# The second layer's seven products: order, transfers and splits set by hand, and small copies ahead of their halves

## The chip, the core and the metric

The kernel runs on one core of a Trainium2 chip. A core has five engines that run side by side, each through its own queue in order: TensorE (PE, matrix products, with weight loads in a sub-queue PEld), VectorE (DVE), ScalarE (ACT), GpSimd (POOL) and SyncE (SP, which here only issues transfers). PE reads SBUF and writes PSUM, eight banks of 128 x 512 fp32; DVE and ACT read the banks. Transfers (DMA) are issued on SP's, POOL's or ACT's queue; those that add to their destination are issued on POOL's. The metric is the device time of one execution in microseconds (us), as a median of several runs.

## The reference

Two layers on x (512 tokens x 1024): a pooling mixer and multi-head latent attention with 16 heads, each gated and projected back, then one RMS norm. What matters here is the second layer's end:

```python
def mla_layer(x, cos, sin, norm_g, w_in, q_norm_g, w_q_b, kv_norm_g, w_kv_b, w_out):
    ...
    o = causal_mla_attention(q_nope, q_rope, k_nope, k_rope, v)
    y = o.reshape(B, S, MLA_WIDTH) * jax.nn.silu(z)
    return x + y @ w_out

def reference(...):
    ...
    return rmsnorm(x, final_norm)
```

`y` is 512 x 2048, `w_out` 2048 x 1024.

## The kernel before

**Precision.** Each fp32 operand is split into a high and a low half (`halves`: ACT copies the rounded value, DVE subtracts it). `mm3` makes one product of three matmuls: high·high, low·high, high·low.

**Attention.** A loop runs over the 16 heads `h`. In the pass of head `h` stand the scores of head `h + 1` (`scores`: per block `i` of 128 queries a bank or part of one, and on DVE a masked row maximum into `mx`), the transposes of head `h`'s weights (`transposes`: three banks, split into `pt_hi`, `pt_lo`; the diagonal corner of keys block 3 is copied whole into `pt_3`), the softmax of head `h + 1`, projections for later heads (`qk`, `vv`) and the values of head `h` (`values`). In `qk` a bank is split into halves and its first 128 columns are also copied whole (`t0`), since block 0 of the scores is made of whole fp32 operands (L988). In `vv` the second bank has such a copy, too (`v3`). Before the change each small copy comes after the halves of its bank. Two engines that read one bank do so one after the other.

**Seven products.** `y @ w_out` is made of seven products in place of eight. `y` (kept transposed) is cut into a11, a12 (first 256 tokens; first and second half of the channels) and a21, a22 (last 256 tokens); `w_out` into B11, B12 (first half of its rows; LEFT and RIGHT columns) and B21, B22. Before, they run in this order:

| | left factor | right factor | banks |
|---|---|---|---|
| 1 | a11 | B11 | `acc` |
| 2 | s1 = a21 − a22 | B11 + B12 (`x_sum`) | `both` |
| 3 | s2 = s1 − a11 | + B22 (`x_sum`) | `acc` |
| 4 | s2 + a12 | B22 (`y_sum`) | `both` |
| 5 | s3 = a11 − a21 | B22 + B12 (`y_sum`) | `acc` |
| 6 | a12 | B21 | `last` |
| 7 | a22 | all four summed (`x_sum`) | `acc` |

Product 1 runs inside the loop, one fourth in each of heads 12 to 15. Each later one is `multiply`: four `part`s of 12 matmuls, the first two with the first strip of the right factor, the last two with the second. `gather` adds a bank to `xs`, the residual rows, between the products that go on in the same bank.

**Sums by transfer.** `Summed.load` loads tiles of `w_out` on SP's queue and adds further quarters to them on POOL's queue. `Summed.strip` then splits a tile set into a strip. A strip takes two of four buffers (tag "w"), so a strip's buffers come free when the product that reads it is half done or done. `x_sum` has eight tiles of 256 KB in buffers of the attention (tags qh, ql, kh, kl): four at head 13 and four at head 14, the latter once the last scores have been made. `y_sum` has four of 512 KB. The left factors' halves lie in two slots that take turns.

**Order.** A planner orders the instructions of each engine by program order and by its own estimate of readiness. Inside `tc.manual_schedule()` each engine takes them as written. Before the change, only `finish` (the squares, norms and the last product's parts) is written under it; the products before it are the planner's.

Of the kernel before, what the change touches and what calls it, by code (L numbers as in the profile page):

```python
# [11 lines left out]
F32 = mybir.dt.float32  # L12
# [3 lines left out]
ALU = mybir.AluOpType  # L16

P = 128
D = 1024
S = 512  # L20
NT = S // P
# [29 lines left out]
def trunk_kernel(  # L51
# [824 lines left out]
    for i in range(3, 8):  # L876
# [13 lines left out]
        base=0,  # L890
# [17 lines left out]
    def projections(p):  # L908

        wq, wkv = strip(pair_parts(p), eng=pool)  # L910
        pairs[p] = st = {}

        def qk(name, i):
            def unit():
                b = bank()
                if name == "q":
                    ws, ks, off = tuple(v[:, :, i * DN : (i + 1) * DN] for v in wq), range(3), 0
                else:
                    ws, ks, off = tuple(v[:, :, i * 256 : i * 256 + DN] for v in wkv), range(2), 3
# [12 lines left out]
                t0 = ap.tile([P, P], F32, name=f"{name}0", tag=f"{name}0", bufs=1)  # L932
                act.activation(t0, b[:, :P], AF.Copy)
                st[name, i] = (th, tl, t0)

            return unit

        def vv(i):
            def unit():
                if i == 0:  # L940
                    st["v"] = tuple(
                        xn_tile(F32R).rearrange("p (t c) -> p t c", t=NT) for n in "hl"
                    )
                b = bank()
                for j in range(2):
# [16 lines left out]
                halves(b[:, : n * 256], vh, vl)  # L962
                if i == 1:
                    st["v3"] = ap.tile([P, 256], F32, name="v3", tag="v3", bufs=1)
                    act.activation(st["v3"], b[:, 256:], AF.Copy)

            return unit

        return [[qk("k", 0), qk("q", 0)], [qk("k", 1), qk("q", 1)], [vv(0), vv(1)]]
# [3 lines left out]
    def scores(h):  # L973
# [42 lines left out]
    def transposes(pm):  # L1016
        for keys in ((0,), (1, 3), (2,)):
            b = bank()
            n = 0
            for j in keys:  # L1020
                for i in range(j, NT):
                    pe.transpose(  # L1022
                        b[:, n : n + P], pm[:, OFF[i] + j * P : OFF[i] + (j + 1) * P], ident
                    )
                    n += P
            n, base = (NT - keys[0]) * P, PT_BASE[keys[0]]
            halves(b[:, :n], pt_hi[:, base : base + n], pt_lo[:, base : base + n])
            if 3 in keys:
                act.activation(pt_3, b[:, n:], AF.Copy)

    def values(h):
        st, i2 = pairs[h // 2], h % 2
# [13 lines left out]


    w_out2 = mla_w_out[0]
    a11, a12, a21, a22 = quarters()
    x_sum, y_sum = Summed(w_out2, 1), Summed(w_out2, 2)  # L1050

    def slot_of(hi, lo):
# [2 lines left out]
            for name, (home, tag) in (("a_hi", hi), ("a_lo", lo))  # L1055
        )

    def sum_tiles(n):

        for i in range(n):  # L1060
            tag = ("qh", "ql", "kh", "kl")[i]
            x_sum.tiles.append(ap.tile([P, 1, S], F32, name="b_x", tag=tag, bufs=2))

    (k0, q0), (k1, q1), vs = projections(0)
    qr = {1: QRope(1)}
# [11 lines left out]
    for h in range(H):  # L1077
        p, odd = divmod(h, 2)
        g, t = divmod(h + 5, 4)
        if h == 12:  # L1080
            slots[1] = slot_of((lp, "t2"), (lp, "q_r"))
            first_half[0] = columns_of(w_out2, 0, LEFT, 0)
            split_tokens(a11, slots[1], (0, 1))
            acc = [bank() for _ in range(2)]
        if h == 13:
            split_tokens(a11, slots[1], (2, 3))
        nxt = scores(h + 1) if h + 1 < H else None
        if h in (13, 14):
            sum_tiles(4)
            x_sum.load(0, LEFT, pieces=range(4 * (h - 13), 4 * (h - 12)))  # L1090
            x_sum.load(0, RIGHT, add=True, pieces=range(4 * (h - 13), 4 * (h - 12)))
        if odd:
            ahead = projections(p + 2) if p + 2 < H // 2 else [[], [], []]
        transposes(sc[0])
# [9 lines left out]
        if h == 14:  # L1104
            slots[0] = slot_of((lp, "latT_hi"), (wk, "q_r"))
            s1 = lp.tile([P, 8, 256], F32, name="s1", tag="latT_lo", bufs=1)
            s1 = [s1[:, 2 * i : 2 * i + 2, :] for i in range(4)]
            s2 = [
                lp.tile([P, 2, 256], F32, name="s2", tag=tag, bufs=1)
                for tag in ("cosT", "sinT", "k_a", "k_b")  # L1110
            ]
            combine(s1, a21, a22, ALU.subtract, range(3))
            split_tokens(s1, slots[0], range(2))
        if h == 15:
            t1 = x_sum.strip(0)
            split_tokens(s1, slots[0], (2,))
            combine(s2, s1, a11, ALU.subtract, range(3))
        values(h)
        if g < 4 and t < 2:
            if t == 0:  # L1120
# [10 lines left out]
        sc = nxt  # L1131


    combine(s1, a21, a22, ALU.subtract, (3,))
    split_tokens(s1, slots[0], (3,))
# [4 lines left out]
    y_sum.load(1, RIGHT)  # L1140
    both = [bank() for _ in range(2)]
    t1 = [t1, x_sum.strip(1)]
    x_sum.load(1, RIGHT, add=True)
    multiply(both, t1, slots[0], True)
    for t in range(2):
        gather(t, LEFT, acc[t])
    combine(s2, s1, a11, ALU.subtract, (3,))
    split_tokens(s2, slots[1])
    multiply(acc, x_sum.strips(), slots[1], False)
    x_sum.load(1, LEFT, add=True)  # L1150
    for t in range(2):
        gather(2 + t, RIGHT, both[t])
    combine(s2, s2, a12, ALU.add)
    split_tokens(s2, slots[0])
    for t in range(2):
        gather(t, RIGHT, acc[t], ALU.subtract)
    multiply(both, y_sum.strips(), slots[0], False)
    y_sum.load(0, RIGHT, add=True)
    g_fin = row(final_norm, D, "g_fin", tag="gain")
    s3 = [  # L1160
        v.rearrange("p (i k c) -> p i k c", i=2, k=2)[:, i]
        for v in (xn_tile(), xn_tile())
        for i in range(2)
    ]
    combine(s3, a11, a21, ALU.subtract)
    split_tokens(s3, slots[1])
    for t in range(2):
        gather(t, RIGHT, both[t])
    multiply(acc, y_sum.strips(), slots[1], False)
    split_tokens(a12, slots[0])  # L1170
    last = [bank() for _ in range(2)]
    multiply(last, [columns_of(w_out2, 1, LEFT, i) for i in range(2)], slots[0], True)
# [5 lines left out]
    junk = lp.tile([P, 512], F32, name="junk", tag="turned", bufs=1)  # L1178
    ssq = {t: [] for t in range(NT)}
    rs = {}  # L1180

# [34 lines left out]
        act.activation(o[t][:, c], o[t][:, c], AF.Copy, scale=rs[t])  # L1216
        send(t, c, queue)

    for t in range(2):
        gather(2 + t, RIGHT, acc[t], ALU.subtract)  # L1220
    split_tokens(a22, slots[1])
    t4 = x_sum.strips()

    def finish():

        for t in range(2):
            square(t, RIGHT)
            square(2 + t, RIGHT)
        for t in range(2):
            gather(t, LEFT, last[t])  # L1230
            total(t)
            square(t, LEFT)
            power(t)
        for t in range(2):
# [22 lines left out]
        normed(3, LEFT)  # L1257

    with tc.manual_schedule():
        finish()  # L1260
    phase.close()

# [36 lines left out]
```

## Time and profile before

| | us |
|---|---|
| median of 3 runs | 721.43 |
| lowest, highest | 720.68, 722.55 |
| the profiled execution | 719.77 |
| its span, first to last instruction | 717.9 |
| PE busy | 701.2 |
| DVE busy | 450.9 |
| ACT busy | 353.6 |
| POOL busy | 137.4 |

The loop over heads starts at about 443 us, product 2 at 641, product 7 at 699.6; PE's last matmul starts at 710.5. In the profile a matmul of 512 columns is shown with 0.39 us, though the next one starts 0.23 us behind it, because matmuls are pipelined. A row of the timeline has start, duration, engine, line, instruction, output and inputs, shapes and a count; in brackets stands the engine's idle time before it and what ended it. A row of the windows has, for each stretch, its length, busy time (and count) of PE, PEld, DVE, ACT, POOL, then the granted clock of PE as a share of full speed, the DMA share and GB/s.

### The profile page before, as it was taken

The page shows a single profiled execution, that of the slowest core. Times are in us where ns is not written, and L with a number is a line of the kernel's source. Part 1 is how long each engine was busy: PE and PEld are TensorE (multiplying, and loading weights), DVE is VectorE, ACT ScalarE, POOL GpSimd, SP SyncE. Part 2 cuts the span into 40 slices and gives each one's busy share as a digit, 9 for nine tenths or more (in the row PEclk, how much of TensorE's full clock was granted, in tenths as well). Part 3 has the DMA queues.
Part 4 walks back from the last instruction along what each step waited for, and adds up shares of the span by engine and source line. Part 5 has one row for each costly group of instructions (what it writes and reads, how often), then busy time and mean ns, then how long its engine had stood idle before and what let it go on. Part 6 is the DMA issues. An engine that isn't in the chain of part 4 may idle for free.

```text
span 717.9 us, 10034 instructions
## 1 busy us (share of the span) xinstructions
PE 701.2 (98%) x3529; PEld 597.8 (83%) x3529; DVE 450.9 (63%) x883; ACT 353.6 (49%) x765; POOL 137.4 (19%) x182
## 2 busy tenths in 40 slices
PE   8999999999999999999999999999999999999896
PEld 7888888888888888799888888898888888877685
DVE  5964453463587897651634212686776887788885
ACT  6462242232243565554642334665575576555662
POOL 5000000000001440154600005221223021054302
PEclk9999999999999999999999999999999999999998
DMA  8341331332355996134432514123132143599813
GB/s 263 120 135 62 115 114 63 118 98 78 111 171 123 238 198 136 57 110 131 118 112 67 155 52 125 53 50 84 53 95 59 38 126 122 114 222 212 153 44 119
DMA packets 69539, 82.79 MB, mean 115 GB/s; under 512 B 12144, under 2 KB 45936, under 8 KB 69488
## 3 DMA queue, kind: packets, MB, share of 16 engines
q1 hardware_dynamic: 60448, 65.10, 30.3%
q0 software_dynamic: 8896, 16.78, 13.3%
q8 instruction: 28, 0.46, 0.3%
q10 hardware_dynamic: 144, 0.26, 0.1%
q14 instruction: 23, 0.19, 0.1%
HBM read 75.83 MB, written 2.10 MB: 109 GB/s over the span
## 4 chain that ended last, share of the span: by engine, by line
PE 87%; DVE 5%; DMA 4%; ACT 2%; issue 1%; POOL 1%; POOLq 0%; SPq 0%; ACTq 0%
PE bank L185 26%; PE bank L184 26%; PE bank L183 26%; DMA b_x<-in_mla_w_out 3%; PE bank L1022 2%; PE bank L301 2%; PE bank L985 2%; PE bank L986 1%; DMA b_y<-in_mla_w_out 1%; DVE a_lo L189 1%; PE bank L988 1%; PE bank L226 1%; ACT pm L1008 1%; DVE pm L1014 1%; DVE w_lo L560 1%
## 5 line engine op out<-in xcount | busy, mean ns | idle before, releaser
L166 ACT ACTIVATE w_hi<-raw 128x512 fp32r<-128x512 f32 (+2 forms) x200 | 105.0, 576 | 130.0 <-PE bank L184 119.7
L167 DVE TENSOR_TENSOR w_lo<-raw,w_hi 128x512 fp32r<-128x512 f32 x132 | 86.6, 691 | 114.0 <-ACT w_hi L166 114.0
L183 PE MATMUL bank<-h_hi,w_hi 128*128 128x512 f32 x368 | 143.6, 390 | 0.0
L185 PE MATMUL bank<-h_lo,w_hi 128*128 128x512 f32 x368 | 143.4, 390 | 0.0
L184 PE MATMUL bank<-h_hi,w_lo 128*128 128x512 f32 x368 | 143.4, 390 | 0.0
L167 POOL TENSOR_TENSOR w_lo<-raw,w_hi 128x256 fp32r<-128x256 f32 (+2 forms) x68 | 61.3, 931 | 193.5 <-ACT w_hi L166 193.4
L185 PEld LDWEIGHTS bank<-h_lo,w_hi 128*128 128x128 f32 x368 | 69.1, 188 | 14.3
L183 PEld LDWEIGHTS bank<-h_hi,w_hi 128*128 128x128 f32 x368 | 69.1, 188 | 14.3
L184 PEld LDWEIGHTS bank<-h_hi,w_lo 128*128 128x128 f32 x368 | 69.1, 188 | 14.2
L183 PE MATMUL bank<-w_hi,h_hi 128*128 128x512 f32 (+1 forms) x176 | 64.6, 367 | 0.0
L184 PE MATMUL bank<-w_hi,h_lo 128*128 128x512 f32 (+1 forms) x176 | 64.2, 365 | 0.0
L185 PE MATMUL bank<-w_lo,h_hi 128*128 128x512 f32 (+1 forms) x176 | 64.2, 365 | 0.0
L185 PE MATMUL bank<-w_lo,a_hi 128*128 128x512 f32 (+1 forms) x116 | 44.7, 386 | 2.8 <-DVE w_lo L560 2.8
L183 PE MATMUL bank<-w_hi,a_hi 128*128 128x512 f32 (+1 forms) x116 | 44.6, 385 | 0.0
L184 PE MATMUL bank<-w_hi,a_lo 128*128 128x512 f32 (+1 forms) x116 | 44.5, 383 | 0.0
L559 ACT ACTIVATE w_hi<-b_x 128x512 fp32r<-128x512 f32 (+1 forms) x40 | 30.6, 798 | 24.8 <-DMA b_x<-in_mla_w_out 9.3
L183 PE MATMUL bank<-latT_hi,w_hi 128*128 128x512 f32 x104 | 42.3, 407 | 0.0
L185 PE MATMUL bank<-latT_lo,w_hi 128*128 128x512 f32 x104 | 40.7, 391 | 0.0
L184 PE MATMUL bank<-latT_hi,w_lo 128*128 128x512 f32 x104 | 40.7, 391 | 0.0
L992 DVE CUSTOM_DVE_ANT_0 pm<-bank,mask 128x128 f32<-128x128 f32 (+2 forms) x64 | 30.5, 489 | 14.8 <-PE bank L185 10.7
L560 DVE TENSOR_TENSOR w_lo<-b_x,w_hi 128x512 fp32r<-128x512 f32 (+1 forms) x40 | 34.3, 902 | 6.1 <-ACT w_hi L559 5.9
L185 PEld LDWEIGHTS bank<-w_lo,h_hi 128*128 128x128 f32 x176 | 33.1, 188 | 4.4
(204 smaller groups left out, 1405.7 us busy)
## 6 DMA issues: line engine op xcount, KB each, us to landing
raw<-in_pool_w_in SPq DMA_DIRECT2D x64, 256.0 KB, 3.1
raw<-in_mla_w_in SPq DMA_DIRECT2D x32, 256.0 KB, 3.3
b_x<-in_pool_w_out POOLq DMA_DIRECT2D x12, 512.0 KB, 7.5
b_x<-in_mla_w_out POOLq DMA_DIRECT2D x24, 256.0 KB, 7.9
raw<-in_mla_w_q_b SPq DMA_DIRECT2D x36, 128.0 KB, 2.4
raw<-in_pool_w_group SPq DMA_DIRECT2D x16, 256.0 KB, 2.6
q_r<-stack SPq DMA_DIRECT2D x64, 64.0 KB, 2.0
raw<-in_mla_w_kv_b SPq DMA_DIRECT2D x16, 256.0 KB, 2.9
```

The source lines that it names most:

```text
L166: act.activation(hi, raw, AF.Copy)
L167: ins = eng.tensor_tensor(lo, raw, f32(hi), ALU.subtract)
L183: pe.matmul(o, a[0], b[0], start=start, stop=False, skip_group_check=more)
L184: pe.matmul(o, a[1], b[0], start=False, stop=False, skip_group_check=more)
L185: pe.matmul(o, a[0], b[1], start=False, stop=stop, skip_group_check=more)
L189: dve.tensor_tensor(lo, src, f32(hi), ALU.subtract)
L301: pe.matmul(first[i][:, c], w0.views[0][a][:, k, i * P : (i + 1) * P], (h_hi, h_lo)[b][:, k, c], start=k == 0 and n == 0, stop=k == KD - 1 ...
L559: act.activation(hv[:, k, :], raw, AF.Copy)
L560: eng.tensor_tensor(lv[:, k, :], raw, f32(hv[:, k, :]), ALU.subtract)
L985: pe.matmul(o, q_r[h // 4][:, h % 4, c], k_a[:, :n], start=True, stop=False)
L992: dve.tensor_tensor_reduce(out=pm[:, OFF[i] : OFF[i] + w], in0=o[:, :w], in1=mask[:, S - w :], scale=1.0, scalar=-3.0e38, op0=ALU.add, op1 ...
L1022: pe.transpose(b[:, n : n + P], pm[:, OFF[i] + j * P : OFF[i] + (j + 1) * P], ident)
```

## The change

Four things change.

- In `qk`, `vv` and `transposes` the small whole copy on ACT comes ahead of `halves`.
- `scores` takes the blocks in the order 1, 2, 3, 0.
- Products 2 to 7 are written in `products()`, under `manual_schedule` together with `finish`, in the order 2, 6, 3, 4, 5, 7 of the table. s3 and s2 are formed in place, in a21's and a11's storage, rows 0 to 5 ahead of the block and rows 6 and 7 in it. Splits take four rows (1024 columns) at a time, combines two.
- The sum tiles of `x_sum` lie in qh, ql, kh, kl, and three buffers that the rotary tables and their work had (cosT, sinT, turned): seven are loaded at head 13 and one at head 14. `finish` makes the norms of the first 256 tokens ahead of the gathers that product 7 waits for.

```diff
             def unit():  # qk; likewise vv and transposes
...
-                halves(b[:, c0:], th[:, c0:], tl[:, c0:])
                 t0 = ap.tile([P, P], F32, name=f"{name}0", tag=f"{name}0", bufs=1)
                 act.activation(t0, b[:, :P], AF.Copy)
+                halves(b[:, c0:], th[:, c0:], tl[:, c0:])
...
-        for i in range(NT):
+        for i in (1, 2, 3, 0):
...
+    homes = [(ap, tag, 2) for tag in ("qh", "ql", "kh", "kl")]
+    homes += [(lp, tag, 1) for tag in ("cosT", "sinT", "turned")]
+    homes += [(ap, "qh", 2)]
+    def first_sum(k0, k1):
+        for home, tag, n in homes[k0:k1]:
+            x_sum.tiles.append(home.tile([P, 1, S], F32, name="b_x", tag=tag, bufs=n))
+        x_sum.load(0, LEFT, pieces=range(k0, k1))
+        x_sum.load(0, RIGHT, add=True, pieces=range(k0, k1))
...
+        if h == 13:
+            first_sum(0, 7)
+        if h == 14:
+            first_sum(7, 8)
...
+            combine_rows(s1, a21, a22, ALU.subtract, 0, 6)
+            split_rows(s1, slots[0], 0, 4)
         if h == 15:
+            t1 = [x_sum.strip(0)]
+            split_rows(s1, slots[0], 4, 6)
...
+    combine_rows(a21, a11, a21, ALU.subtract, 0, 6)
+    combine_rows(a11, s1, a11, ALU.subtract, 0, 6)
+    s3, s2 = a21, a11
...
+    def products():
+        combine_rows(s1, a21, a22, ALU.subtract, 6, 8)
+        split_rows(s1, slots[0], 6, 8)
+        x_sum.load(1, RIGHT, add=True, pieces=range(4))
+        t1.append(x_sum.strip(1))
+        x_sum.load(1, RIGHT, add=True, pieces=range(4, 8))
+        multiply(both, t1, slots[0], True)
+        split_rows(a12, slots[1], 0, 4)
+        p2 = [columns_of(w_out2, 1, LEFT, 0)]
+        split_rows(a12, slots[1], 4, 8)
+        p2.append(columns_of(w_out2, 1, LEFT, 1))
+        y_sum.load(1, RIGHT)
+        multiply(last, p2, slots[1], True)
+        for t in range(2):
+            gather(t, LEFT, acc[t])
+            gather(2 + t, RIGHT, both[t])
+        combine_rows(s3, a11, a21, ALU.subtract, 6, 8)
+        combine_rows(s2, s1, a11, ALU.subtract, 6, 8)
+        split_rows(s2, slots[0], 0, 4)
+        split_rows(s2, slots[0], 4, 8)
+        t2 = x_sum.strips()
+        x_sum.load(1, LEFT, add=True)
+        multiply(acc, t2, slots[0], False)
+        for i in (0, 4):
+            combine_rows(s2, s2, a12, ALU.add, i, i + 4)
+            split_rows(s2, slots[1], i, i + 4)
+        y1 = [y_sum.strip(0)]
+        for t in range(2):
+            gather(t, LEFT, last[t])
+        y1.append(y_sum.strip(1))
+        y_sum.load(0, RIGHT, add=True)
+        multiply(both, y1, slots[1], False)
+        for t in range(2):
+            gather(t, RIGHT, acc[t], ALU.subtract)
+        split_rows(s3, slots[0], 0, 4)
+        split_rows(s3, slots[0], 4, 8)
+        y2 = [y_sum.strip(0)]
+        for t in range(2):
+            gather(t, RIGHT, both[t])
+        y2.append(y_sum.strip(1))
+        multiply(acc, y2, slots[0], False)
+        split_rows(a22, slots[1], 0, 4)
+        split_rows(a22, slots[1], 4, 8)
...
     def finish():
+        t4 = [x_sum.strip(0)]
         for t in range(2):
+            square(t, LEFT)
+            total(t)
             square(t, RIGHT)
-            square(2 + t, RIGHT)
-        for t in range(2):
-            gather(t, LEFT, last[t])
-            total(t)
-            square(t, LEFT)
             power(t)
-        for t in range(2):
-            part(acc[t], t4[0], slots[1], 0, t, False, False, True)
             for c in (LEFT, RIGHT):
                 normed(t, c)
+        for t in range(2):
+            gather(2 + t, RIGHT, acc[t], ALU.subtract)
+            square(2 + t, RIGHT)
+            part(acc[t], t4[0], slots[1], 0, t, False, False, True)
+        t4.append(x_sum.strip(1))
         part(acc[0], t4[1], slots[1], 1, 0, False, True, True)
...
     with tc.manual_schedule():
+        products()
         finish()
```

`combine_rows` works on two rows (512 columns) an instruction, `split_rows` on all the rows that it is given.

More of the change, by code (lines that the diff above doesn't have):

```diff
@@ L961, in unit @@
                 )
-                halves(b[:, : n * 256], vh, vl)
                 if i == 1:
@@ L965, in unit @@
                     act.activation(st["v3"], b[:, 256:], AF.Copy)
+                halves(b[:, : n * 256], vh, vl)
             return unit
@@ L1026, in transposes @@
             n, base = (NT - keys[0]) * P, PT_BASE[keys[0]]
-            halves(b[:, :n], pt_hi[:, base : base + n], pt_lo[:, base : base + n])
             if 3 in keys:
                 act.activation(pt_3, b[:, n:], AF.Copy)
+            halves(b[:, :n], pt_hi[:, base : base + n], pt_lo[:, base : base + n])
     def values(h):
@@ L1048, in trunk_kernel, with combine_rows, split_rows @@
     w_out2 = mla_w_out[0]
-    a11, a12, a21, a22 = quarters()
+    a11, a12, a21, a22 = (
+        y[:, half * 8 : half * 8 + 8, t * 256 : (t + 1) * 256] for t in range(2) for half in range(2)
+    )
+    def combine_rows(out, a, b, op, k0, k1):
+        for k in range(k0, k1, 2):
+            dve.tensor_tensor(*(v[:, k : k + 2, :] for v in (out, a, b)), op)
+    def split_rows(src, slot, k0, k1):
+        halves(*(v[:, k0:k1, :] for v in (src, *slot)))
     x_sum, y_sum = Summed(w_out2, 1), Summed(w_out2, 2)
@@ L1056, in slot_of @@
         )
[L1058 to L1062, printed above, removed]
+    homes = [(ap, tag, 2) for tag in ("qh", "ql", "kh", "kl")]
[6 more added lines that the diff above has]
+        x_sum.load(0, RIGHT, add=True, pieces=range(k0, k1))
     (k0, q0), (k1, q1), vs = projections(0)
@@ L1082, in trunk_kernel @@
             first_half[0] = columns_of(w_out2, 0, LEFT, 0)
-            split_tokens(a11, slots[1], (0, 1))
+            split_rows(a11, slots[1], 0, 4)
             acc = [bank() for _ in range(2)]
         if h == 13:
-            split_tokens(a11, slots[1], (2, 3))
+            split_rows(a11, slots[1], 4, 8)
         nxt = scores(h + 1) if h + 1 < H else None
[L1088 to L1091, printed above, removed]
+        if h == 13:
+            first_sum(0, 7)
+        if h == 14:
+            first_sum(7, 8)
         if odd:
@@ L1106, in trunk_kernel @@
             s1 = lp.tile([P, 8, 256], F32, name="s1", tag="latT_lo", bufs=1)
[L1107 to L1113, printed above, removed]
+            combine_rows(s1, a21, a22, ALU.subtract, 0, 6)
+            split_rows(s1, slots[0], 0, 4)
         if h == 15:
-            t1 = x_sum.strip(0)
-            split_tokens(s1, slots[0], (2,))
-            combine(s2, s1, a11, ALU.subtract, range(3))
+            t1 = [x_sum.strip(0)]
+            split_rows(s1, slots[0], 4, 6)
         values(h)
@@ L1131, in trunk_kernel @@
         sc = nxt
-    combine(s1, a21, a22, ALU.subtract, (3,))
-    split_tokens(s1, slots[0], (3,))
+    combine_rows(a21, a11, a21, ALU.subtract, 0, 6)
+    combine_rows(a11, s1, a11, ALU.subtract, 0, 6)
+    s3, s2 = a21, a11
     y_sum.tiles = [
@@ L1139, in trunk_kernel @@
     ]
-    y_sum.load(1, RIGHT)
     both = [bank() for _ in range(2)]
-    t1 = [t1, x_sum.strip(1)]
-    x_sum.load(1, RIGHT, add=True)
-    multiply(both, t1, slots[0], True)
-    for t in range(2):
[L1146 to L1150, printed above, removed]
-    for t in range(2):
-        gather(2 + t, RIGHT, both[t])
-    combine(s2, s2, a12, ALU.add)
-    split_tokens(s2, slots[0])
@@ L1155, in trunk_kernel @@
[L1155 to L1158, printed above, removed]
-    g_fin = row(final_norm, D, "g_fin", tag="gain")
[L1160 to L1169, printed above, removed]
@@ L1170, in trunk_kernel @@
-    split_tokens(a12, slots[0])
-    last = [bank() for _ in range(2)]
-    multiply(last, [columns_of(w_out2, 1, LEFT, i) for i in range(2)], slots[0], True)
+    last = [bank() for _ in range(2)]
+    g_fin = row(final_norm, D, "g_fin", tag="gain")
+    def products():
[41 more added lines that the diff above has]
+        split_rows(a22, slots[1], 4, 8)
@@ L1177, in trunk_kernel @@
     ]
-    junk = lp.tile([P, 512], F32, name="junk", tag="turned", bufs=1)
+    junk = lp.tile([P, 512], F32, name="junk", tag="k_a", bufs=1)
     ssq = {t: [] for t in range(NT)}
```

6 lines of the change are left out of this document (removed).

## The prediction

> **What bounds the kernel now.** I read the page first, then TensorE's (PE's) waits, then the timelines of single engines around each wait.
>
> ```profile
> span 717.9 us, 10034 instructions
> ...
> PE 701.2 (98%) x3529; PEld 597.8 (83%) x3529; DVE 450.9 (63%) x883; ACT 353.6 (49%) x765; POOL 137.4 (19%) x182
> ```
>
> PE is busy 701.2 of 717.9 us. The change adds and drops no matrix product, so it can only touch the 16.7 us in which PE stands. Some 7 us of them lie behind PE's last matmul, which ends at 710.77 (its row stands below with the clock), in a stage that the change leaves in order. The start takes 3.5 (12.00 − 8.53 in its window, first fence here), and the waits in between stand in the second (engine and line; whom it waited for; us, times, longest):
>
> ```profile
> 0.00:12.00 12.00, 8.53 (x39) 7.30 (x40) 5.08 (x12) 7.00 (x17) 5.43 (x16) 1.00 0.85 276
> ```
> ```profile
> PE bank L185 <- DVE w_lo L560: 2.8, 3, 1.7
> PE bank L988 <- ACT q L933: 1.6, 3, 0.5
> PE bank L1044 <- ACT pt L1029: 1.1, 1, 1.1
> ```
>
> Of the waits the first lies in the seven products, the second in the loop over heads, the third at its end. PE's timeline (start, duration, instruction, idle before it) has the places:
>
> ```profile
> 537.89 0.49 PE L988 MATMUL bank<-k,q 128*128 128x128 f32 x2 [0.52 <-ACT q L933]
> 641.06 0.49 PE L1044 MATMUL bank<-pt,v 128*128 128x128 f32 x2 [1.05 <-ACT pt L1029]
> 653.44 0.50 PE L185 MATMUL bank<-w_lo,a_hi 128*128 128x512 f32 x1 [0.51 <-DVE w_lo L560]
> 664.22 0.39 PE L184 MATMUL bank<-w_hi,a_lo 128*128 128x512 f32 x1
> 666.27 0.50 PE L185 MATMUL bank<-w_lo,a_hi 128*128 128x512 f32 x1 [1.67 <-DVE w_lo L560]
> 666.61 0.39 PE L183 MATMUL bank<-w_hi,a_hi 128*128 128x512 f32 x1
> 678.14 0.50 PE L185 MATMUL bank<-w_lo,a_hi 128*128 128x512 f32 x1 [0.67 <-DVE w_lo L560]
> 699.58 0.39 PE L183 MATMUL bank<-w_hi,a_hi 128*128 128x512 f32 x1
> 707.51 0.39 PE L185 MATMUL bank<-w_lo,a_hi 128*128 128x512 f32 x1
> ```
>
> From 699.58 to 707.51 are 35 steps of 0.227 us: PE's pitch. A product of 48 matmuls takes 10.88 us. Starts 664.22 and 666.61 are two steps apart and should differ by 0.45; they differ by 2.39, so that wait costs 1.94, its idle time plus 0.27. With the same surcharge the waits at 653.44 and 678.14 cost 0.78 and 0.94, the one at 641.06 1.3, each of the three at L988 about 0.75.
>
> Behind the waits in the products stand transfers; the chain of waits has them in order of time (start, us):
>
> ```profile
> 635.84 8.67 DMA b_x<-in_mla_w_out
> 649.11 7.98 DMA b_x<-in_mla_w_out
> 666.76 5.97 DMA b_y<-in_mla_w_out
> ```
>
> Each is an adding transfer that can start only when the sum before it has been split, and that the next product needs at once. Four of eight sum tiles also get their buffers late, at head 14.
>
> **The change part by part.** *Transfers and the product order.* Putting a12·B21, whose weights come plain from memory, second-next gives the B22 addition a whole product (10.88 us) more, against 7.98 us of transfer. Seven of eight sum tiles are loaded at head 13 instead of four, so the second strip no longer waits for the 8.67. The addition for the second sum starts with the fourth product's first splits and is needed a product later: 10.9 us against 5.97. So the three DMA-fed waits go: −(0.78 + 1.94 + 0.94) = −3.66.
>
> What is late next is DVE, cleared of its transfers:
>
> ```profile
> 650.29 2.50 DVE L189 TENSOR_TENSOR a_lo<-s,a_hi 128x512 fp32r<-128x512 f32 x4
> 666.73 3.50 DVE L560 TENSOR_TENSOR w_lo<-b_y,w_hi 128x1024 fp32r<-128x1024 f32 x3
> 663.35 2.93 ACT L559 ACTIVATE w_hi<-b_y 128x1024 fp32r<-128x1024 f32 x3
> ```
>
> So 0.60 us on DVE for 512 columns, 1.15 for 1024, and 0.97 on ACT for 1024. The tightest place is from the start of product s2·(sum) to the product after it: DVE does, in the hand order, four strip pieces 2.4, two combines 1.2, a split 1.15, two combines 1.2, a split 1.15, and the next strip's first piece 1.15: 8.25. Both splits first wait for ACT's copy of what DVE has just combined, 2 × 1.05, and the first piece waits 0.55 for ACT: 10.9. The next product's first use of a low half is at 10.88 + 0.45 = 11.33. Slack 0.4; I take a wait of 0.2, bounds 0 and 0.8.
>
> Larger splits (1024 in place of two of 512) save 0.05 of 1.2; the extra combines before the products fill DVE's gaps at the loop's end. I cost both at nothing: the cover is the 5.4 us of the second product's first half, which needs only rows split at head 14. Without it, up to 1.8 us (three combines of 0.60) would show.
>
> *The new wait.* The old closing order read the accumulators with the right-half sums ahead of everything; the new one puts four scalings of finished rows (L1207) on DVE ahead of the two gathers that free the accumulators for the last product, which now directly follows a product into the same banks. Rows of the old closing stage:
>
> ```profile
> 694.11 2.20 ACT L559 ACTIVATE w_hi<-b_x 128x512 fp32r<-128x512 f32 x4 [0.74 <-PE bank L184]
> 688.29 0.63 ACT L1184 ACTIVATE junk<-xs 128x512 f32<-128x512 f32 x1 [2.34 <-DVE xs L610]
> 699.11 0.57 POOL L1201 TENSOR_TENSOR rs<-rs,mhalf 128x1 f32<-128x1 f32 x1
> 702.51 0.42 POOL L1200 TENSOR_TENSOR rs<-ssq,total 128x1 f32<-128x1 f32 x1 [2.52 <-ACT junk L1184]
> 703.00 0.96 POOL L1201 TENSOR_TENSOR rs<-rs,mhalf 128x1 f32<-128x1 f32 x1
> 702.79 2.74 DVE L1207 SCALAR_TENSOR_TENSOR o<-xs,rs,g_fin 128x512 f32<-128x512 f32 x4
> 709.37 0.69 DVE L610 TENSOR_TENSOR xs<-xs,bank 128x512 f32<-128x512 f32 x1
> ```
>
> Count from the start of the sixth product. The product before the last one began at 699.58 − 10.88 = 688.70 and ACT could fill the next strip at 694.11, 5.41 later, since a half-used strip gives its buffers up only then. ACT: strip 5.41 to 7.6; four squares of 0.63 to 10.1. POOL's sum and power of the second row tile follow: 0.9 with the fast rows, 1.5 with the slow ones (POOL beside a working DVE, as at 702.51), up to 0.8 more if the first tile's are slow too: 11.0 to 12.4. DVE: the first tile's two scalings (1.37) are done by about 11.5, the second tile's take 1.37 more, to 12.5 to 13.8; the gather 0.69: 13.2 to 14.5. PE was ready at 10.88. Loss 2.4 to 3.6; I take **+2.9**, nearer the slow rows because here, too, POOL runs beside DVE. Behind the gather stand the second gather, two squares and the last strip, needed 5.4 us later; they take about 4.5. The sends, seven on SP, have nothing else to wait for there.
>
> *The small copies and the score order.*
>
> ```profile
> 533.36 0.28 ACT L1029 ACTIVATE pt<-bank 128x128 f32<-128x128 f32 x1
> 537.56 0.28 ACT L933 ACTIVATE q<-bank 128x128 f32<-128x128 f32 x1 [0.19 <-DVE ql L189]
> 536.98 0.55 DVE L189 TENSOR_TENSOR ql<-bank,qh 128x384 fp32r<-128x384 f32 x1
> 639.70 1.15 ACT L559 ACTIVATE w_hi<-b_x 128x512 fp32r<-128x512 f32 x2 [1.20 <-DMA b_x<-in_mla_w_out]
> 640.75 0.26 ACT L1029 ACTIVATE pt<-bank 128x128 f32<-128x128 f32 x1
> ```
>
> ACT's small copy waits for DVE's half of the same bank. At 640.75 it also stands behind copies that wait for a transfer. Ahead of the halves it needs neither: −1.3 at L1044, hidden then by the value product's first nine matmuls. At L988 the q copy comes 0.6 us earlier, but ql ends at 537.53 and the next matmul needs it by about 537.4; it moves forward by some 0.3 since the copy at 533.36 leaves the row of exponentials, and the reordered scores put L988 last. I take −0.5 for each of three: −1.5, bounds 0 and −2.25.
>
> Sum: −3.66 + 0.2 + 2.9 − 1.3 − 1.5 = **−3.4 us**. The profiled execution took 719.77 us (717.9 and 1.9 around the span), which gives 716.4; it lay 1.66 below the median of the runs, 721.43, so the forecast is **718.1**.
>
> **The rivals.** *The clock falls in the new wait.*
>
> ```profile
> 710.49 0.28 PE L185 MATMUL bank<-w_lo,a_hi 128*128 128x256 f32 x1
> 713.00:713.50 0.50, 0.00 (x0) 0.00 (x0) 0.34 (x1) 0.34 (x1) 0.12 (x1) 1.00 0.88 336
> 713.50:714.00 0.50, 0.00 (x0) 0.00 (x0) 0.41 (x1) 0.38 (x1) 0.00 (x0) 0.54 0.51 189
> ```
>
> The last-but-two column is PE's granted clock: half from 713.54 on, 2.8 us after PE's last matmul ended (710.77). The new wait leaves PE idle for about 2.2 to 3.5 us. At half clock each us costs 0.5; the trace shows no return. If it takes as long to come back as to go (2.8 us, an estimate), 1.4: 719.5. Ends 0 and, for the whole last product, 10.9. The Trainium skill, "TensorE: Matmul & The Clock Gate", Part 1, says that an idle window of about 3.4 us halves the clock and as much sustained work restores it; by it 1.7 us would be lost, and only where a window falls wholly into the wait. The trace's drop after 2.8 us is shorter than that rule.
>
> *The loop gives nothing.* The planner sets the loop's order outside the manual block, so the three stalls may stay as ql's: +1.5 to the sum, 719.6. For it speaks 537.53 against 537.4.
>
> *The other side: the longer row of maxima.*
>
> ```profile
> 626.17 0.28 DVE L992 CUSTOM_DVE_ANT_0 pm<-bank,mask 128x128 f32<-128x128 f32 x1
> 626.38 0.09 DVE L992 DVE_READ_ACCUMULATOR2_ANT mx<- 128x1 f32 x1
> ```
>
> With block 0 last, 0.36 us stand between the widest block's maximum and the exponentials, in each of 16 heads. If PE's cover is as thin as in the three heads that stall, that is 16 × 0.36 = +5.8 in place of −1.5: 725.3. It turns the result slower from 0.26 per head. Against it: the wide block's matmuls then end earlier by block 0's own PE time, and thirteen heads show no stall.
>
> *No new wait*, if squares and scalings come earlier than I count: 715.2. In the old trace the hand-ordered closing instructions stand in exactly the written order on each engine, which speaks against it.
>
> **How the numbers follow.** The measurement tells about 0.3% from no change, here 2.2 us: faster is below 719.3. Chances: forecast 0.52 (its own bounds 716.5 to 719.9, 0.44 of it faster), no new wait 0.12 (faster), clock 0.12 (0.04 faster), loop gives nothing 0.14 (0.04 faster), longer maxima 0.10 (slower). Faster 0.64, same 0.26, slower 0.10. The range, 715.0 to 721.0, leaves out the slower case and about half of the lowest.
>
> **What would show it.** Right: no wait of L1044 on L1029 and none of L988 on L933; no DMA in PE's waits after 640; one PE idle of 2 to 3.5 us just ahead of the last product, ended by a DVE xs gather. Wrong: that gap missing, a granted clock under 1.00 after it, new waits on w_lo L560 at the fourth product, or PE waiting for scores or transposes in heads that had no stall.

## The result and the profile after

The changed kernel takes 726.03 us (median of 6 runs, 724.54 to 727.53) where the kernel before takes 720.93: ratio 1.0069, 95% interval 1.0049 to 1.0090. It is slower by 0.7%. The forecast was 718.1 with a range to 721.0, so the sign was wrong. The six runs lie in two groups, 724.5 to 725.1 and 727.0 to 727.5, so a median of few runs can move by 1 us with their mix, and the profile shows one of the faster group. The profiled execution has a span of 723.3 us where before had 717.9.

The waits of PE in the profile after (engine and line; whom it waited for; us, times, longest):

```profile
PE bank L183 <- DVE xs L610: 5.1, 1, 5.1
PE bank L183 <- ACT w_hi L559: 2.0, 1, 2.0
...
PE bank L185 <- DVE w_lo L560: 0.6, 1, 0.6
```

L988 and L1044 are gone from the list, and so are the three waits on w_lo of before, which a sum by transfer fed. PE now waits at two other places. PE's timeline after (start, duration, instruction, idle before it):

```profile
659.66 0.39 PE L185 MATMUL bank<-w_lo,a_hi 128*128 128x512 f32 x1
662.05 0.50 PE L183 MATMUL bank<-w_hi,a_hi 128*128 128x512 f32 x1 [2.00 <-ACT w_hi L559]
...
663.39 0.80 PE L185 MATMUL bank<-w_lo,a_hi 128*128 128x512 f32 x1 [0.61 <-DVE w_lo L560]
663.99 0.63 PE L183 MATMUL bank<-w_hi,a_hi 128*128 128x512 f32 x1
...
666.42 0.40 PE L183 MATMUL bank<-w_hi,a_hi 128*128 128x512 f32 x1
...
697.16 0.39 PE L185 MATMUL bank<-w_lo,a_hi 128*128 128x512 f32 x1
702.69 0.77 PE L183 MATMUL bank<-w_hi,a_hi 128*128 128x512 f32 x1 [5.14 <-DVE xs L610]
703.25 0.63 PE L184 MATMUL bank<-w_hi,a_lo 128*128 128x512 f32 x1
...
707.40 0.40 PE L185 MATMUL bank<-w_lo,a_hi 128*128 128x512 f32 x1
```

The first place is the start of product 3 (s2 times the sum), which is now the third that is computed there. Its matmul at 666.42 is the tenth behind 659.66; at the pitch of 0.227 it would start at 661.93. The place costs 4.5 us. The second place is the start of product 7: the matmul at 707.40 is the twelfth behind 697.16, due at 699.88. It costs 7.5 us. Behind both waits a matmul takes 0.63 and starts 0.43 after the one before, about twice the usual pitch: the clock is halved, as the windows after say (length, busy time of PE, PEld, DVE, ACT, POOL, granted clock, DMA share, GB/s):

```profile
663.00:666.00 3.00, 2.61 (x6) 2.13 (x7) 3.00 (x6) 2.64 (x6) 2.37 (x4) 0.50 0.15 24
...
704.00:705.00 1.00, 1.00 (x4) 0.72 (x4) 0.33 (x1) 1.00 (x4) 0.00 (x0) 0.50 0.00 0
```

The balance: 12.0 us lost at the two places. Gained were 3.66 at the old waits on w_lo, 1.3 at L1044 and 3 × 0.75 at L988, together 7.2. The difference is +4.8; the spans differ by 5.4 and the medians by 5.1. PE's rows at the bounds of the stages (the loop's first scores, product 2, PE's last matmul; first before, then after) give the 5.4 by stages:

```profile
444.15 0.28 PE L985 MATMUL bank<-k_a,q_r 128*128 128x256 f32 x1
641.30 0.48 PE L183 MATMUL bank<-w_hi,a_hi 128*128 128x512 f32 x1
710.49 0.28 PE L185 MATMUL bank<-w_lo,a_hi 128*128 128x256 f32 x1
```
```profile
444.60 0.28 PE L985 MATMUL bank<-k_a,q_r 128*128 128x256 f32 x1
638.63 0.48 PE L183 MATMUL bank<-w_hi,a_hi 128*128 128x512 f32 x1
715.88 0.28 PE L185 MATMUL bank<-w_lo,a_hi 128*128 128x256 f32 x1
```

The loop is 3.1 us shorter (197.15 to 194.03), where its waits alone give 3.5. Products 2 to 7 are 8.1 us longer (69.19 to 77.25), where the places give 12.0 − 3.66 = 8.3. The stretch ahead of the loop was 0.45 longer in this execution.

**What stands behind the first place.** The order after on ACT and DVE (timeline, two engines):

```profile
654.04 1.84 ACT L166 ACTIVATE w_hi<-raw 128x512 fp32r<-128x512 f32 x3 [4.47 <-DMA raw<-in_mla_w_out]
...
660.42 1.06 ACT L188 ACTIVATE a_hi<-y 128x1024 fp32r<-128x1024 f32 x1 [3.59 <-DVE y L1055]
```
```profile
654.71 1.90 DVE L167 TENSOR_TENSOR w_lo<-raw,w_hi 128x512 fp32r<-128x512 f32 x3 [4.19 <-ACT w_hi L166]
656.53 2.47 DVE L610 TENSOR_TENSOR xs<-xs,bank 128x512 f32<-128x512 f32 x4
```

Three of the eight weight tiles of product 6 (a12 times B21, which reads its weights plain) land 7 us after their issue. PE itself does not need them sooner. But DVE is held by them for 4.2 us, and the four gathers, two combines and the splits that product 3 needs are written behind them.

**What stands behind the second place.** ACT is held by the sum of `y_sum`, then DVE by the scalings (ACT's and DVE's timeline after):

```profile
688.21 1.06 ACT L559 ACTIVATE w_hi<-b_y 128x1024 fp32r<-128x1024 f32 x1 [1.56 <-DMA b_y<-in_mla_w_out]
690.67 1.06 ACT L559 ACTIVATE w_hi<-b_y 128x1024 fp32r<-128x1024 f32 x1 [1.40 <-DMA b_y<-in_mla_w_out]
...
693.53 2.18 ACT L559 ACTIVATE w_hi<-b_x 128x512 fp32r<-128x512 f32 x4
```
```profile
698.39 1.41 DVE L1233 SCALAR_TENSOR_TENSOR o<-xs,rs,g_fin 128x512 f32<-128x512 f32 x2 [0.73 <-POOL rs L1227]
700.54 1.41 DVE L1233 SCALAR_TENSOR_TENSOR o<-xs,rs,g_fin 128x512 f32<-128x512 f32 x2 [0.73 <-POOL rs L1227]
701.87 1.28 DVE L610 TENSOR_TENSOR xs<-xs,bank 128x512 f32<-128x512 f32 x2
```

The last product's first strip reaches ACT at 693.53, 7.0 us after product 5 began (697.39 − 10.88 = 686.51) where the forecast had 5.41. Then come the squares, POOL, four scalings, and only then the gather that frees the bank.

### The profile page after: what moved, and what is told of

Same layout as the page of the kernel before. It is cut to its first block, busy times and chain, and to the rows that moved or that the text cites. A ratio compares the mean times of both kernels' runs of the same rounds, so it can differ in the third digit from the quotient of the medians.

```text
span 723.3 us, 10067 instructions
## 1 busy us (share of the span) xinstructions
PE 704.1 (97%) x3529; PEld 601.6 (83%) x3529; DVE 444.9 (62%) x870; ACT 348.0 (48%) x752; POOL 138.4 (19%) x182
## 4 chain that ended last, share of the span: by engine, by line
PE 88%; issue 4%; POOL 3%; DMA 2%; DVE 1%; ACT 1%; POOLq 0%; SPq 0%; ACTq 0%; DVEq 0%
PE bank L183 26%; PE bank L184 26%; PE bank L185 26%; PE bank L1022 2%; PE bank L301 2%; POOL b_x L546 1%; PE bank L986 1%; PE bank L985 1%; DMA b_y<-in_mla_w_out 1%; PE bank L226 1%; PE bank L1044 0%; PE bank L988 0%; DMA xs<-in_x 0%; PE bank L271 0%; POOL b_y L546 0%
## 5 line engine op out<-in xcount | busy, mean ns | idle before, releaser
L183 PE MATMUL bank<-w_hi,a_hi 128*128 128x512 f32 (+1 forms) x116 | 46.3, 399 | 7.1 <-DVE xs L610 5.1
L546 POOL DMA_DIRECT2D b_x<-in_mla_w_out x24 | 21.5, 1416 | 86.3 <-DVE w_lo L560 26.2
L183 PEld LDWEIGHTS bank<-w_hi,h_hi 128*128 128x128 f32 x176 | 33.0, 188 | 4.4
```

What stands on the lines that cost most here:

```text
L183: pe.matmul(o, a[0], b[0], start=start, stop=False, skip_group_check=more)
L546: pool.dma_start(self.tiles[i], src, accum_op=ALU.add)
```

## The experiments

The theory after the result: the loop's part is worth about what was forecast, and all of the loss lies at the two places, each a queue held in its written order by a late transfer or by work that could wait. The rivals for each place are in the expectations. Every run was timed against the kernel before on the same chip; its median was 720.2 to 721.4 us. "Changed" is the changed kernel, 726.0 us, ratio 1.0069.

| run | base and edit | us | ratio to before, 95% |
|---|---|---|---|
| a1 | changed; gathers ahead of squares and scalings | 719.17 | 0.9982, 0.9968 to 0.9997 |
| a2 | changed; 12 spare matmuls in the last wait | 726.55 | 1.0077, 1.0058 to 1.0095 |
| a6 | changed; 20 spare matmuls | 723.71 | 1.0046, 1.0030 to 1.0061 |
| a7 | changed; a22's splits ahead of the late strip | 724.01 | 1.0039, 1.0023 to 1.0055 |
| a4 | changed; gathers and combines ahead of the late weights | 722.62 | 1.0023, 1.0011 to 1.0036 |
| a3 | changed; plain `y_sum` loads first | 726.59 | 1.0079, 1.0059 to 1.0099 |
| a5 | changed; plain `y_sum` loads last | 726.14 | 1.0064, 1.0045 to 1.0082 |
| a8 | changed; four adding transfers later, new tile | 733.29 | 1.0183, 1.0168 to 1.0198 |
| a9 | the same without a new tile | 723.87 | 1.0040, 1.0026 to 1.0054 |
| b1 | before; small copies first | 719.62 | 0.9971, 0.9956 to 0.9985 |
| b2 | before; scores 1, 2, 3, 0 | 717.07 | 0.9938, 0.9916 to 0.9960 |
| b3 | before; both | 718.33 | 0.9954, 0.9938 to 0.9971 |
| c1 | a1 and a4 | 716.35 | 0.9927, 0.9902 to 0.9951 |
| c2 | a1, a4 and a7 | 715.87 | 0.9919, 0.9896 to 0.9943 |
| c3 | a1, a7 and a8 | 725.16 | 1.0074, 1.0057 to 1.0090 |
| c4 | a1, a7 and a9 | 716.73 | 0.9948, 0.9933 to 0.9962 |

### The last product's wait: a1, a7, a2, a6

```diff
 def finish():  # a1
     t4 = [x_sum.strip(0)]
+    for t in range(2):
+        gather(2 + t, RIGHT, acc[t], ALU.subtract)
     for t in range(2):
         square(t, LEFT)
...
     for t in range(2):
-        gather(2 + t, RIGHT, acc[t], ALU.subtract)
         square(2 + t, RIGHT)
```

> Base is the changed kernel. The two gathers that free the accumulators stand ahead of the four scalings (L1233 there) in the closing stage; nothing else differs. Theory (the scalings ahead of the gathers make the wait before the last product): PE's 5.14 us idle before the last product falls to about 0.9 (DVE is then held only by the late strip), the clock stays at 1.00 there, and about 6.4 us come back: 719.6 us. Rival (the wait is made by the late second sum, whatever stands on DVE): at most the 2.8 us of scalings come back, the clock still falls: 722 to 724.

In a1 PE's timeline has, ahead of the last product, only this:

```profile
699.04 0.47 PE L183 MATMUL bank<-w_hi,a_hi 128*128 128x512 f32 x1 [0.32 <-DVE xs L610]
```

5.14 us became 0.32, and 0.9% came back (1.0069 to 0.9982, about 6.3 us). The work written ahead of the gathers made this wait: the squares, the norms on POOL and the scalings. Its rival, that the late sum alone makes it, falls. How much the late sum adds to it was asked by a7:

```diff
+        split_rows(a22, slots[1], 0, 4)
+        split_rows(a22, slots[1], 4, 8)
         y2.append(y_sum.strip(1))
         multiply(acc, y2, slots[0], False)
-        split_rows(a22, slots[1], 0, 4)
-        split_rows(a22, slots[1], 4, 8)
```

> Base is the changed kernel. The two splits of a22 stand ahead of the second strip of the fifth computed product, whose summed transfer lands late; the scalings stay ahead of the gathers. Theory (of the 5.14 us before the last product some 1.6 come from ACT being held by that late sum, the rest from the scalings): the wait falls to about 3.4 us, the clock still falls: 724.3. Rival (the scalings and POOL alone set it): 5.1 us and 726.0.

```profile
702.05 0.56 PE L183 MATMUL bank<-w_hi,a_hi 128*128 128x512 f32 x1 [3.55 <-DVE xs L610]
```

5.14 became 3.55: with the gathers still last, 1.6 us of the wait came from ACT being held by the late sum, the rest from the work ahead of the gathers. The time, 724.0, is near the expected 724.3, but it does not measure the 1.6 by itself: in a7's profile the clock did not fall at product 3, as it did in the changed kernel's.

In a2 and a6 PE makes spare matmuls in that wait, into a bank that nobody reads (12 are one more `part`, 20 are eight matmuls more).

```diff
         multiply(acc, y2, slots[0], False)
+        part(bank(), y2[1], slots[0], 1, 1, True, True, False)
```

> Base is the changed kernel. PE makes 12 more matmuls (2.7 us) into a spare bank that nobody reads, between the fifth computed product and the last one, so it idles some 2.4 us in place of 5.14 while everything else waits as before. Theory (the clock falls because PE idles over 2.8 us, and the halved clock costs 2 us on top of the wait): the granted clock stays 1.00 in the last product and the time falls by 2.1 to 723.9 us. Rival (the clock falls for another reason, or the slow matmuls are hidden by the wait for the next strip): no change, 726.0.

> Base is the changed kernel. PE makes 20 matmuls (4.5 us) into a spare bank that nobody reads ahead of the last product, in place of the 12 that left it idle for 2.65 us and still lost the clock; now some 0.7 us of idle time stay. Theory (idling halves the clock, and that costs 2 us on top of the wait): granted clock 1.00 in the last product, 726.0 - 2.1 = 723.9 us. Rival (the slow matmuls cost nothing, since the next strip sets the pace): clock 1.00 and 726.0.

a2 missed: with 2.65 us of idle time left the clock fell just as PE began again, and the time did not move. In a6 (PE's timeline; the first row is the last spare matmul) 0.84 us are left:

```profile
702.27 0.39 PE L1208 MATMUL bank<-w_hi,a_lo 128*128 128x512 f32 x1
703.49 0.47 PE L183 MATMUL bank<-w_hi,a_hi 128*128 128x512 f32 x1 [0.84 <-DVE xs L610]
...
706.11 0.39 PE L185 MATMUL bank<-w_lo,a_hi 128*128 128x512 f32 x1
```

The first twelve matmuls of the last product take 2.62 us from start to start (703.49 to 706.11), in the changed kernel 4.71 (702.69 to 707.40). So the halved clock cost 2.1 us there, on top of the wait. The total fell by 0.23% (1.7 us), but in this profile the clock did not fall at the first place either, so the total alone does not split the two.

### The first place: a4, a5, a3, a8, a9

```diff
         split_rows(a12, slots[1], 4, 8)
+        for t in range(2):
+            gather(t, LEFT, acc[t])
+            gather(2 + t, RIGHT, both[t])
+        combine_rows(s3, a11, a21, ALU.subtract, 6, 8)
+        combine_rows(s2, s1, a11, ALU.subtract, 6, 8)
         p2.append(columns_of(w_out2, 1, LEFT, 1))
```

(a4; the same six lines go from behind `multiply(last, ...)`.)

> Base is the changed kernel. The four gathers and two combines that follow a12's product in the written order stand ahead of the second strip of that product's weights, whose transfer is late; the transfer itself is left as it is. Theory (DVE, in order behind the late strip, is what makes PE wait 2.0 + 0.6 us and lose the clock before the third computed product): those 3.7 us of DVE work fit into the 4.2 us in which DVE stood, PE's waits there go, 4.5 us come back: 721.5. Rival (the split of s2 or its buffers, not DVE's queue, set the start): under 1 us comes back.

PE's waits of 2.00 and 0.61 are gone from a4's timeline, and 0.46% (3.3 us) came back of 4.5; the expectation had 721.5. The weights land as late as before (ACT's timeline of a4):

```profile
654.62 1.84 ACT L166 ACTIVATE w_hi<-raw 128x512 fp32r<-128x512 f32 x3 [4.25 <-DMA raw<-in_mla_w_out]
```

So it was DVE's queue behind them that made PE wait. Part of what is missing is a wait at the next product, which the slow start of product 3 had hidden (a4):

```profile
672.98 0.50 PE L185 MATMUL bank<-w_lo,a_hi 128*128 128x512 f32 x1 [0.71 <-DVE w_lo L560]
```

The last product's wait is also somewhat longer there, 5.43 us.

Why do the weights land late? Two groups of transfers lie next to them: four adding ones of `x_sum`, issued just before, and four plain ones of `y_sum`, just behind. a5 moves the plain ones away:

```diff
-        y_sum.load(1, RIGHT)
+        for i, tl in enumerate(y_sum.tiles):
+            act.dma_start(tl, w_rows(w_out2, 8 + 2 * i, 2)[:, :, RIGHT])
```

> Base is the changed kernel. The four plain loads of y_sum are issued on ACT's queue, behind ACT's last copies of a12's weights, so that they start only when those weights have landed; the adding transfers stay where they are. Theory A (the plain loads hold the three weight loads up): the weights land 3 to 4 us after issue in place of 7.0, DVE is not held, PE's 2.0 + 0.6 us before the third computed product go with the drop of the clock: 721.5 us. Theory B (the adding transfers hold them up): 7 us to landing and 726 us as before.

The weights still took 6.3 us to landing, the time stayed at 726.1: the plain loads are not what holds them. a3 puts the plain loads first instead (`y_sum.load(1, RIGHT)` as the first line of `products`):

> Base is the changed kernel. The four plain loads of y_sum (2 MB) are issued first in the block in place of right behind the last three weight loads of a12's product. Theory A (these loads share the transfer engines with the three weight loads and hold them up): the weights land 3 to 4 us after issue in place of 7.0, PE's waits before the third computed product go, 4.5 us come back: 721.5. Theory B (the adding transfers issued just before hold them up): they land as late as before, 726.0.

It is of little use: on SP's queue the loads waited for buffers, and all eight weight loads stood behind them. The weights took 6.4 to 7.7 us to landing, the time was 726.6. a8 and a9 move the adding transfers: POOL first reads one column of ACT's last copy of the weights.

```diff
-        x_sum.load(1, RIGHT, add=True, pieces=range(4, 8))
         multiply(both, t1, slots[0], True)
...
         p2.append(columns_of(w_out2, 1, LEFT, 1))
+        mark = sm.tile([P, 1], F32, name="mark")  # a9: name="ssq"
+        pool.tensor_copy(mark, f32(p2[1][0][:, 3, :1]))
+        x_sum.load(1, RIGHT, add=True, pieces=range(4, 8))
```

> Base is the changed kernel. The four adding transfers of x_sum (tiles 4 to 7) are issued only when ACT has copied the last of a12's weights: POOL reads one column of that copy first. Everything else stays. Theory B (the adding transfers hold up the three weight loads): the weights land some 3 us after issue in place of 7.0, DVE is not held for 4.2 us, PE's waits of 2.0 + 0.6 us before the third computed product go: 721.5 us. Rival (three loads of 256 KB need that long by themselves, or beside y_sum's plain loads, which are then issued next to them): 6 us or more to landing and about 726 us.

> As a8_adds_late, but the one column that POOL reads goes into a tile that exists already (ssq), so that no buffer of the kernel moves in SBUF: in a8 the extra tile moved the others and the matmuls of the whole program became 2% slower (395 in place of 389 ns). Theory B (the adding transfers hold up the weights): the three weight loads land in about 3.5 us as in a8, PE's waits before the third computed product go, 721.5 us. Rival: what a8 gained at that place is paid elsewhere, 724 to 726.

The landing times of the three weight loads, in the changed kernel and in a9 (min, median, max):

```profile
DMA to landing us min/median/max: 6.9/7.0/7.0
```
```profile
DMA to landing us min/median/max: 2.4/3.9/3.9
```

But for POOL's small read only the adding transfers differ between the two, so they held the weights up. In a9 PE does not wait at product 3. The time is 723.9 and not 721.5, nearly the rival's 724: the additions now come so late that the next product starts late (1.65 and 0.72 us idle at 672.80 and 674.25). In a8 the three loads landed after 2.4 to 4.9 us, but its time says nothing of the place: its new tile cost some 8 us ahead of the loop (last section).

### The loop: b1, b2, b3

```diff
+                t0 = ap.tile([P, P], F32, name=f"{name}0", tag=f"{name}0", bufs=1)  # b1; likewise in vv, transposes
+                act.activation(t0, b[:, :P], AF.Copy)
                 halves(b[:, c0:], th[:, c0:], tl[:, c0:])
-                t0 = ap.tile([P, P], F32, name=f"{name}0", tag=f"{name}0", bufs=1)
-                act.activation(t0, b[:, :P], AF.Copy)
...
-        for i in range(NT):  # b2
+        for i in (1, 2, 3, 0):
```

> Base is the kernel before. Only the small copies go ahead of their halves. Theory (ACT's wait for DVE's read of the same bank makes PE's waits at L988 and L1044): the 1.05 us wait on L1029 and the three of 0.52 on L933 go, -1.3 and -1.5 to -2.25: 717.4 to 718.1 where before is 720.9. Rival (the low half of q is as late as the copy): L1044 goes, the three stay in part, -1.3: 719.6.

> Base is the kernel before. Only the blocks of the scores are taken in the order 1, 2, 3, 0. Theory: block 0, the one that needs the small copies, comes last, so the three waits on L933 go and L1044's stays: -1.5 to -2.25, 718.7 to 719.4. Rival (the row of maxima gets longer by 0.36 us a head and the planner has no cover): new PE waits for scores or transposes, up to +5.8: 726.7.

> Base is the kernel before. Small copies first and the new block order together, products and transfers as before. Theory: the loop's part of the change is worth -3.5 (1.3 at L1044, 2.25 at L988): 717.4. Rival: 719.6, if only L1044's wait goes.

All three are faster than before, by 2.1, 4.5 and 3.3 us by their ratios, and in none does PE wait at L988 or L1044. The rival of the longer row of maxima falls: b2 shows no new wait for scores or transposes. b1's way shows in ACT's waits: between 440 and 645 us the kernel before has

```profile
ACT k L933 <- DVE kl L189: 13.1, 11, 1.5
ACT q L933 <- DVE ql L189: 5.6, 13, 1.6
```

and b1 has neither. In b2 both stay (11.6 and 5.5 us), only the scores no longer need the copies first. That b2 also loses the wait at L1044 was not expected. Its ACT makes the same copies in the same order as before, but the first two do not wait for a transfer, where before they waited 1.20 us:

```profile
636.87 1.16 ACT L559 ACTIVATE w_hi<-b_x 128x512 fp32r<-128x512 f32 x2
637.93 0.26 ACT L1029 ACTIVATE pt<-bank 128x128 f32<-128x128 f32 x1
```

Why the transfer is in time there was not followed up. The gains in time miss the expectations both ways: b1 gave 2.1 us, between its rival's 1.3 and its theory's 2.8 to 3.5, though its waits went as the theory says; b2 gave 4.5, where its theory had 1.5 to 2.25. Part of the gain is given back at once: the next wait on a DMA-fed strip grows from 1.67 us to 2.35, 2.72 and 3.04 in b1, b2 and b3, and in all three profiles the clock is halved near it, which it is not before (b3's row):

```profile
664.87 0.79 PE L185 MATMUL bank<-w_lo,a_hi 128*128 128x512 f32 x1 [3.04 <-DVE w_lo L560]
```

PE begins product 2 earlier, at 638.47 to 639.06 in place of 641.30, by 2.2 to 2.8 us; the strip comes only 1.3 to 2.0 us earlier (664.32 to 664.96 in place of 666.27). The intervals of b2 and b3 overlap, so which is better is open.

### Together: c1, c2, c3, c4

> Base is the changed kernel. The gathers stand ahead of the scalings in the closing stage, and the sums after a12's product stand ahead of its second strip (the two edits of the first two places in one). Theory (the two places are independent and hold all that was lost): both waits and both drops of the clock go, 726.0 - 4.5 - 6.4 = 715.1. Rival (mending the first place brings the last product nearer to the second sum's transfers, whose end is set by their own 10 us): the last wait grows by what the first gives back and the sum is 718 to 720.

> Base is the changed kernel. All three edits of order: sums ahead of the late weights' strip, a22's splits ahead of the late sum's strip, gathers ahead of the scalings. Theory (the places are independent): the 1.06 us that stayed before the last product with the first two edits go, 716.35 - 1.3 = 715.0 us, and no drop of the clock before PE's last matmul. Rival (DVE is full there anyway): no difference from 716.35.

> Base is the changed kernel. The later adding transfers in place of the moved sums, with a22's splits ahead of the late strip and the gathers ahead of the scalings. Theory (two ways to the same end): PE's waits before the third computed product and before the last one are gone, 715 to 716 us, the same as with three edits of order (715.87). Rival: if the weights land late all the same, some 4 us more, 719 to 720.

> As c3_fixes_adds_late, without the moved buffers. Theory: the later adding transfers mend the first place as well as the moved sums do, 715 to 716 us. Rival: 719 to 720, if some of the wait stays.

c1, the two edits of order, takes 1.4% off the changed kernel; c2 with all three is the fastest of all, 715.87 us, 0.8% below before (1.0 to 0.6%). What a1 and a4 gave one by one adds up in c1 (6.3 and 3.3 us, together 1.3%), so the two places are nearly independent. Not wholly: in c1 the last product waits 1.06 us where a1 left 0.32, as c1's rival had it, and its time, 716.35, lies between the theory's 715.1 and the rival's 718. c2's difference from c1 lies inside their intervals. So mended, the change pays, but much of that is the loop: b2 and b3 alone have ratios of 0.9938 and 0.9954, and the intervals of b2 and c2 overlap. In c2's trace products 2 to 7 take 67.2 us from first to last start (638.31 to 705.54), 2.0 less than before. The waits that are left in c2's products:

```profile
672.00 0.50 PE L185 MATMUL bank<-w_lo,a_hi 128*128 128x512 f32 x1 [0.71 <-DVE w_lo L560]
...
684.87 0.50 PE L185 MATMUL bank<-w_lo,a_hi 128*128 128x512 f32 x1 [0.29 <-DVE w_lo L560]
689.47 0.50 PE L185 MATMUL bank<-w_lo,a_hi 128*128 128x512 f32 x1 [0.18 <-DVE w_lo L560]
```

The late additions of c4 mend the first place, too, but not better (0.9948); c3 carries a8's new tile.

## Why the prediction was wrong

- **"So the three DMA-fed waits go", −3.66: right** in its outcome. None of them is left, and product 6 in second place covers the additions of `x_sum`. For `y_sum` the reason given, 10.9 us against 5.97, was wrong (below: 14.5); that PE does not wait there is in part luck: each tile is split as it lands (ACT's rows at 688.21 and 690.67).
- **The step that failed** stands just before that: weights that "come plain from memory" were given no cost. They run beside the additions, with the DMA share at 1.01 from 650 to 652 us, and landed after 7 us where at most 3.9 is what they take without them (a9); so they held DVE with the work for product 3 written behind. The tightest place of DVE was sought one product later, where 0.2 was forecast with a bound of 0.8; there 0.71 shows once product 3 starts in time (a4, c2). The first place cost 4.5 us and had no term in the sum; that is half of the 8.5 us between the forecast's −3.4 and the measured +5.1.
- **The new wait, +2.9: the mechanism was right, the size was not.** a1 confirms the work ahead of the gathers. The wait was 5.14 us of idle time, and 7.5 us with the clock, 4.6 more than forecast. Of that 1.6 us is the late second sum (a7): the forecast took 5.97 us, one transfer's time, for four that follow one another; from the first issue at 676.15 to the last landing at about 690.7 they took 14.5. The trace before had this already. There the first of the four is issued at 666.76, and ACT waits for the last until 680.46, 13.7 us later:

```profile
680.46 1.06 ACT L559 ACTIVATE w_hi<-b_y 128x1024 fp32r<-128x1024 f32 x1 [1.41 <-DMA b_y<-in_mla_w_out]
```

The 3.55 us that a7 leaves lie at the upper end of the forecast's 2.4 to 3.6.
- **The clock** stood as a rival with 0.12 and a price of 1.4 us. It came at both places; at the last it cost 2.1 us (a6). At the last product it fell in every profile with 2.65 us of idle time or more (the changed kernel, a2 to a5, a7 to a9) and in none with 1.06 or less (a1, a6, c1). The Trainium skill, "TensorE: Matmul & The Clock Gate", Part 1, speaks of an idle window of about 3.4 us and as much work to come back. The wait at product 3 was shorter, 2.0 us and another 0.6, and the clock fell all the same. The way back agrees at this place: the half clock lasted from about 662.9 to 666.2, 3.4 us. In a1 it lasted from about 662.6 to 669.5 at the same place, 6.8 us.
- **The small copies and the score order, −2.8 together: right.** All of the wait at L988 went, not two thirds (b1 to b3), and the loop is 3.1 us shorter.
- **The chance of slower, 0.10,** was put on the loop, where nothing was lost. The two real losses were of one kind, work in a hand-set queue behind something late, and the forecast priced only one of them.

## What to carry to other kernels

When an order is set by hand, follow each engine's queue, not only the chain of the result: at each instruction that waits for a transfer, list what is written behind it and who needs that. Put what frees an accumulator ahead of what only finishes an output. A transfer's time next to other transfers has to be taken from a stretch where these run side by side, and several in a row count as a sum.

## What the runs showed of the hardware

Adding transfers move half as much as plain ones while they keep the engines as busy. Two windows of the changed kernel, the first with additions only (of `y_sum`), the second with plain loads only (the last two columns are DMA share and GB/s):

```profile
680.00:682.00 2.00, 2.00 (x11) 1.65 (x10) 2.00 (x4) 0.00 (x0) 1.91 (x2) 1.00 1.11 200
...
656.00:658.00 2.00, 2.00 (x10) 1.65 (x9) 2.00 (x5) 0.83 (x1) 0.00 (x0) 1.00 1.05 395
```

The clock can fall after PE has begun again. In b2 PE idled 2.72 us and went on at 664.32; the clock was halved from about 665.8 to 669.2 (the last-but-two column):

```profile
664.00:665.00 1.00, 0.68 (x3) 0.60 (x4) 1.00 (x3) 0.33 (x1) 0.19 (x1) 1.00 0.57 102
665.00:666.00 1.00, 1.00 (x6) 0.79 (x5) 1.00 (x2) 0.00 (x0) 1.00 (x1) 0.88 0.00 0
```

Single idle times of 2.35, 2.65, 2.72 and 3.04 us (b1, a2, b2, b3) all brought it, 1.67 (before) did not. At product 3 it fell after 2.0 us and up to 0.6 more in the changed kernel, a1, a2 and a3, and after 1.47 and 0.61 in a5; it did not after 1.9 to 2.0 and 0.61 in a6 and a7, nor at the next product after 1.65 and 0.72 in a9. So the idle time alone does not decide, and what does is open. Up to PE's last matmul, the half clock lasted about 3.4 or 6.8 us each time.

The program's start has it, too. In the profiles of a2 to a5, a7 to a9 and b3 the clock was halved for 3.4 or 6.8 us between about 8.6 and 16.2 us, in the others not. The first scores start at 444.15 in the kernel before and at 446.28 in a5, so part of the scatter between runs may come from there.

A tile of one column per partition, in a pool opened ahead of that of the weight buffers, slowed a part of the matmuls (a8): those of h_hi with the weights went from a mean of 390 ns to 395. The groups by form on PE, in the changed kernel and in a8:

```profile
L183 PE MATMUL bank<-h_hi,w_hi 128*128 128x512 f32 x368 | 143.4, 390 | 0.0
```
```profile
L183 PE MATMUL bank<-h_hi,w_hi 128*128 128x512 f32 x368 | 145.4, 395 | 0.0
```

Others kept theirs (latT_hi with the weights 408 in both). The loss lies ahead of the loop: the first scores start at 453.31 in c3, with the tile, and at 445.25 in c4, without it, 8.1 us apart; from there to product 2 both take 194.0 to 194.1. The edit with the column in an old tile (a9) has 390 again, so the new tile is the cause; that it acts by moving other buffers in SBUF is likely, but not shown. The expectation of a9 has 2% on the matmuls of the whole program; the rows give 1.3% on these and nothing on others.
